# Delta rule on one Trainium2 core: the heads' inverses in groups of two, three and three heads in place of two groups of four

## The chip, the cores and the metric

The kernel runs on one core of one Trainium2 chip. The metric is the device time of one execution in microseconds (us), the median of several runs. The engines are PE (TensorE, matmuls), DVE (VectorE), ACT (ScalarE), POOL (GpSimd) and SP (SyncE, which issues all the DMAs of this kernel). Each engine executes its own instructions in the order in which the program holds them, and waits on semaphores for the others.

## What is computed

One inference step of a 4-layer encoder (pooling mixer, gated DeltaNet, stick-breaking attention, pooling mixer, each followed by a convolutional FFN) for two request groups that share the weights: 512 prompt frames and 64 frames of a running stream, 576 columns in all, in float32. The change lies in the DeltaNet mixer, which has 8 heads of width 128 and works in chunks of 64 frames:

```python
gc = jnp.cumsum(g, axis=-1)
kb = k * beta[..., None]
m = jnp.einsum('nbhid,nbhjd->nbhij', kb, k) * decay_strict
rhs = jnp.concatenate([v * beta[..., None], kb * jnp.exp(gc)[..., None]], axis=-1)
sol = lax.linalg.triangular_solve(eye + m, rhs, left_side=True, lower=True, unit_diagonal=True)
u, w = sol[..., :DV], sol[..., DV:]

def step(s, xs):
    u_c, w_c, qg_c, kg_c, attn_c, gl_c = xs
    v_new = u_c - jnp.einsum('bhck,bhkv->bhcv', w_c, s)
    o_c = jnp.einsum('bhck,bhkv->bhcv', qg_c, s) + jnp.einsum('bhij,bhjv->bhiv', attn_c, v_new)
    s = s * gl_c[..., None, None] + jnp.einsum('bhck,bhcv->bhkv', kg_c, v_new)
    return s, o_c
```

The kernel solves the triangular system by inverting `eye + m`. It takes the prompt in chunks of 128 frames (four) and the running stream in one of 64; the matrix of a chunk is cut into blocks of 32x32 on the diagonal, which are inverted on POOL, and larger inverses are put together from them by matmuls.

## The kernel before

**Planner.** The program is written by a planner (`Flow`) while it is built. Each piece of work is a Python generator that yields what it needs (tiles, free buffers, named events) and then emits instructions. `Flow.run` keeps a modelled clock for each engine and always goes on with the ready generator of the best priority. The order that results is fixed for PE, DVE, ACT, POOL and SP, and the chip executes it as written. A generator that yields `"@G"` is taken up again when POOL's modelled clock is within 250 ns, so that its POOL instructions come between those of others.

**The delta stage** (`dn`, from L1181) runs from about 440 us to 880 us of the span. A worker of the lowest priority emits 32 projections, matmuls of the normed input (split in a high and a low part) with a weight column block, in the order of the string `TN['order']` (L275): k0 q0 q1 k1 k2 q2 k3 q3 v2 v0 v1 v3 k4 q4 k5 k6 q6 k7 q5 q7 z1 z0 z2 z3 v5 v4 v6 v7 z4 z5 z7 z6. What else is ready goes between them:

- `conv` (L1313) follows every k, q and v projection: a memset and a copy on POOL for the first columns, an evacuation of PSUM on DVE, a scaling on ACT, two small copies of the last columns to `dn_so` on POOL, three taps on DVE (`a<-a,dn_cw,a`, 128x579), a tanh on ACT that overwrites the input, and a product on DVE.
- `mat(h)` (L1372) follows the conv of k: k times k on PE, norms and decays, the matrix M. SP stores its diagonal blocks into the DRAM tile `dM[g]` of the group and the whole of it into `Mt[h]`, seven DMAs, and the event `M{h}` is fired.
- `inverse(g)` (L1415) waits for the matrices of its four heads and for two of the eight `h` buffers (the weights use the same ones). It loads the 72 blocks of the group (18 a head) with a block on each partition, sets T to the unit matrix on POOL, and makes 31 steps of forward substitution, two POOL instructions each (a product into a `q` tile, a subtraction from T). ACT writes the transposed T, SP stores both, and `inv{g}` is fired.
- `merge(h)` (L1446) waits for `inv{g}`, loads the head's blocks in 16 DMAs and makes the full inverse U with 22 matmuls of 128 columns. Two U tiles exist at a time (class limit U), and one merge runs at a time (class limit mg).
- `v_post(h)` (L1486) turns v round after its conv; two results exist at a time (class limit v), kept until the end of `rec(h)`.
- `prep_rec(h)` (L1504) makes the decayed attention matrix and keys; it waits for the end of `rec(h-2)`.
- `rec(h)` (L1539) makes the recurrence over the five chunks, one head after the other with some overlap: it needs `prep_rec(h)`, U and v of its head.

The z projections gate the results, and the output projection follows. The trace puts nearly every instruction on L26, the line of the helper that calls the engine, so that groups are told apart by tiles: `h<-h,q` and `q<-h,h` on POOL are the steps of `inverse`, `dn_so<-a` the small copies of `conv`, `d<-a` on SP the stores of `mat`, `b` on DVE a finished k or q, `p` is PSUM.

Of the kernel before, what the change touches and what calls it, by code (L numbers as in the profile page):

```python
# [12 lines left out]
AF = mybir.ActivationFunctionType  # L13
ALU = mybir.AluOpType
# [275 lines left out]
class Step:  # L290
# [890 lines left out]
    def dn(self,l,st,nst,gnext):  # L1181
# [166 lines left out]
        def qk_post(h,i):  # L1348
            def g(P):
                if h not in kq:  # L1350
                    kq[h]=None
                    yield [("b",1)]
                    kq[h]=self.b().rearrange("p (l n) -> p l n",l=2)
                    f.fire(f"{st}:kq{h}")
                else: yield [f"{st}:kq{h}"]
                d=kq[h][:,i]
                c,C=yield from conv((8+h,h)[i],P,d)
                f.free(c)
                if i==0:
                    f.free(C)  # L1360
                    f.spawn(mat(h),TN['mat'])
                    return
                yield [d[:,:579],"@A"]
                A.activation(C[:,:579],d[:,:579],AF.Square)
                q=yield from sums(C,SO)
                f.free(C)
                V.tensor_scalar(out=eq[:,h],in0=q[:,:5],scalar1=4e-6,scalar2=1.28e-4,op0=ALU.add,op1=ALU.mult)
                f.free(q)
                f.fire(f"{st}:qn{h}")
            return g  # L1370

        def mat(h):  # L1372
            k=kq[h][:,0]
            yield [k[:,:579],("a",1,"M"),("p",2),("t",1)]
            M=self.a(cls="M"); r=self.s([128,5],F32,"t",8)
            p=self.p(); q=self.p()
            G.memset(r,1.0)
            for c in range(4): mm(p[:,cc[c]],k[:,cc[c]],k[:,cc[c]],start=True,stop=True)
            mm(q[:64,:64],k[:,ss],k[:,ss],start=True,stop=True)
            yield [p,q[:64,:64],r,"@V"]  # L1380
            for c in range(4): V.scalar_tensor_tensor(out=M[:,cc[c]],in0=p[:,cc[c]],scalar=1.0,in1=self.ident,op0=ALU.mult,op1=ALU.mult,accum_out=r[:,c:c+1])
            V.scalar_tensor_tensor(out=M[:64,sm],in0=q[:64,:64],scalar=1.0,in1=self.ident[:64,:64],op0=ALU.mult,op1=ALU.mult,accum_out=r[:64,4:5])
            V.tensor_scalar(out=r,in0=r,scalar1=4e-6,scalar2=None,op0=ALU.add)
            V.reciprocal(out=rk2[:,h],in_=r)
            G.tensor_tensor(out=r,in0=r,in1=mhalf,op=ALU.pow)
            yield [f"{st}:dec",("p",1)]
            p2=self.p()
            G.memset(M[64:128,sm],0.0)
            bank(h,self.mpos,p2,q,64)
            yield [r,rk2[:,h]]  # L1390
            V.tensor_tensor(out=nbk[:,h],in0=nbe[:,:,h],in1=rk2[:,h],op=ALU.mult)
            V.tensor_tensor(out=vsc[:,h],in0=beta[:,:,h],in1=r,op=ALU.mult)
            f.free(r)
            f.fire(f"{st}:kn{h}")
            yield [p2,q[:64,64:128],"@A"]
            for c in range(4): A.activation(M[:,cc[c]],p2[:,cc[c]],AF.Exp,scale=-1.0,bias=bE[:,c,h:h+1])
            A.activation(M[:64,sm],q[:64,64:128],AF.Exp,scale=-1.0,bias=bE[:64,4,h:h+1])
            f.free(p2)
            yield [M[:,:NT],"@V"]
            for c in range(4): V.scalar_tensor_tensor(out=M[:,cc[c]],in0=p[:,cc[c]],scalar=rk2[:,h,c:c+1],in1=M[:,cc[c]],op0=ALU.mult,op1=ALU.mult)  # L1400
            V.scalar_tensor_tensor(out=M[:64,sm],in0=q[:64,:64],scalar=rk2[:64,h,4:5],in1=M[:64,sm],op0=ALU.mult,op1=ALU.mult)
            f.free(p,q)
            g=h//4; o=18*(h%4)
            if g not in dM: dM[g]=self.dram([72,32,32])
            d=dM[g]
            yield [M[:,:NT]]
            for b in range(4):
                S.dma_start(out=d[o:o+16].rearrange("(c b) i j -> b i c j",b=4)[b],
                    in_=M[32*b:32*b+32,:512].rearrange("p (c j) -> p c j",j=128)[:,:,32*b:32*b+32])
            for b in range(2): S.dma_start(out=d[o+16+b],in_=M[32*b:32*b+32,512+32*b:544+32*b])  # L1410
            Mt[h]=self.dram([128,NT]); S.dma_start(out=Mt[h],in_=M[:,:NT])
            f.free(M)
            f.fire(f"{st}:M{h}")

        def inverse(g):  # L1415
            yield [f"{st}:M{h}" for h in range(4*g,4*g+4)]
            yield [("h",2),("q",1)]
            Bt,Tt=(self._t([128,1024],F32,"h") for _ in (0,1))
            v3=lambda t: t.rearrange("p (i j) -> p i j",j=32)
            MB,T=v3(Bt),v3(Tt)  # L1420
            S.dma_start(out=MB[:72],in_=dM[g])
            G.memset(Tt[:72],0.0); G.memset(Tt[:72,0:1024:33],1.0)
            prt=self.q()
            yield [Bt,Tt]
            for j in range(31):
                yield ["@G"]
                n=31-j; w=j+1
                pr=prt[:72,:n*w].rearrange("p (a b) -> p a b",b=w)
                G.tensor_tensor(out=pr,in0=MB[:72,j+1:,j:j+1].to_broadcast([72,n,w]),in1=T[:72,j:j+1,:w].to_broadcast([72,n,w]),op=ALU.mult)
                G.tensor_tensor(out=T[:72,j+1:,:w],in0=T[:72,j+1:,:w],in1=pr,op=ALU.subtract)  # L1430
            f.free(prt)
            yield [Tt,"@A"]
            A.activation(MB[:72],T[:72].rearrange("p i j -> p j i"),AF.Copy)
            r=[]
            for X in (Tt,Bt):
                d=self.dram([72,32,32])
                yield [X]
                S.dma_start(out=d,in_=X[:72])
                r.append(d)
            f.free(Bt,Tt)  # L1440
            TU[g]=r
            f.fire(f"{st}:inv{g}")
# [1 line left out]


        def merge(h):  # L1446
            g=h//4; hh=h%4
            yield [f"{st}:inv{g}",("a",3,"mg"),("a",1,"U")]
            P=self.a(cls="mg"); U=self.a(cls="U"); T=self.a(cls="mg"); M=self.a(cls="mg")
            for X in (P,U,T,M): G.memset(X[:,:NT],0.0)  # L1450
            D_=Mt.pop(h)
            for i in (0,64): S.dma_start(out=blk(P,0,512)[i+32:i+64,:,i:i+32],in_=blk(D_,0,512)[i+32:i+64,:,i:i+32])
            S.dma_start(out=P[32:64,512:544],in_=D_[32:64,512:544])
            for X,d in ((U,TU[g][1]),(T,TU[g][0])):
                for b in range(4): S.dma_start(out=blk(X,0,512)[32*b:32*b+32,:,32*b:32*b+32],in_=d[18*hh:18*hh+16].rearrange("(c b) i j -> b i c j",b=4)[b])
                for b in (0,1): S.dma_start(out=X[32*b:32*b+32,512+32*b:544+32*b],in_=d[18*hh+16+b])
            S.dma_start(out=blk(M,0,512)[64:128,:,0:64],in_=blk(D_,0,512)[64:128,:,0:64])
            yield [P[:,:NT],U[:,:NT],("p",2)]
            p=self.p(); q=self.p()
            for c in cc: mm(p[:,c],P[:,c],U[:,c],start=True,stop=True)  # L1460
            mm(q[:64,:64],P[:64,sm],U[:64,sm],start=True,stop=True)
            yield [p,q,"@A"]
            A.activation(P[:,:512],p,AF.Copy)
            A.activation(P[:64,sm],q[:64,:64],AF.Copy)
            yield [P,T[:,:NT]]
            for c in cc: mm(p[:,c],T[:,c],P[:,c],start=True,stop=True)
            mm(q[:64,:64],T[:64,sm],P[:64,sm],start=True,stop=True)
            yield [p,q,"@V"]
            V.tensor_tensor(out=U[:64,sm],in0=U[:64,sm],in1=q[:64,:64],op=ALU.subtract)
            V.tensor_tensor(out=U[:,:512],in0=U[:,:512],in1=p,op=ALU.subtract)  # L1470
            for c in cc: mm(q[:,c],P[:,c],T[:,c],start=True,stop=True)
            yield [q,"@V"]
            V.tensor_tensor(out=T[:,:512],in0=T[:,:512],in1=q,op=ALU.subtract)
            f.free(q)
            yield [U,M]
            for c in cc: mm(p[:,c],M[:,c],U[:,c],start=True,stop=True)
            yield [p,"@A"]
            A.activation(P[:,:512],p,AF.Copy)
            yield [P,T]
            for c in cc: mm(p[:,c],T[:,c],P[:,c],start=True,stop=True)  # L1480
            yield [p,"@V"]
            V.tensor_tensor(out=U[:,:512],in0=U[:,:512],in1=p,op=ALU.subtract)
            f.free(p,T,P,M)
            Uf[h]=U
            f.fire(f"{st}:U{h}")
# [164 lines left out]
        def z_(h): proj(24+h,z_post(h),TN['pz'])  # L1650
        for x in TN['order'].split(): dict(k=k_,q=q_,v=v_,z=z_)[x[0]](int(x[1:]))
        def chains():
            for g in (0,1): f.spawn(inverse(g),TN['inv'])
            for h in range(8):
                f.spawn(merge(h),TN['merge']); f.spawn(prep_rec(h),TN['prep']); f.spawn(rec(h),TN['rec'])
        chains()
# [381 lines left out]
```

## Time and profile before

| | us |
|---|---|
| median of 3 runs | 2518.58 |
| lowest and highest | 2518.18 and 2522.79 |
| profiled execution | 2525.03 |
| its span, first to last instruction | 2523.3 |
| PE busy | 2462.4 (98%) |
| PE weight loads busy | 2394.3 (95%) |
| DVE busy | 1924.9 (76%) |
| ACT busy | 1298.2 (51%) |
| POOL busy | 365.9 (15%) |
| mean granted TensorE clock | 0.986 |

Busy time is the union of an engine's instructions; PE's are pipelined, so a busy PE is not PE at its best. The granted clock is 1 at 2.4 GHz and 0.5 at 1.2 GHz. In the trace's views a row with a time begins with the start in us and the duration in us, then engine, line, operation, output<-inputs and the shapes; an idle time before it stands in square brackets with what ended it. A row of a group has, after the bar, the busy time in us and the mean duration in ns, then the idle time before its instructions and what ended it.

### The profile page before, as it was taken

Reading aid. Unit: us, or ns where it says so; the run is one execution under the profiler, and the core shown is the slowest. Engines: PE = TensorE matmul, PEld = TensorE weight load, DVE = VectorE, ACT = ScalarE, POOL = GpSimd, SP = SyncE. Lnnn points to the kernel's source line nnn. Section 1 sums busy time; section 2 is a strip of 40 time slices with the busy share of each in tenths; the row PEclk is TensorE's granted clock in tenths of the full one; section 3 lists DMA queues with packets and bytes.
Section 4 is the critical chain, followed back from the end, with each engine's and each line's share of the span. In section 5 each row is a group of like instructions: output and inputs, shape, how many; then the busy total and the mean of one; then the engine's idle time right before and its main releaser. Section 6 shows DMA issues by size and latency. Waiting matters only on the chain.

```text
span 2523.3 us, 46793 instructions
## 1 busy us (share of the span) xinstructions
PE 2462.4 (98%) x18337; PEld 2394.3 (95%) x18337; DVE 1924.9 (76%) x3727; ACT 1298.2 (51%) x2459; POOL 365.9 (15%) x734
## 2 busy tenths in 40 slices
PE   8989999998999999999999999999999999899998
PEld 7989999998999899999999888899999999899998
DVE  6988787887555479877885767779777788877776
ACT  6455544544344344444565667645444465544445
POOL 0000000138441001000001221200000001000000
PEclk9999999999999999999999999999999999999999
DMA  3223223332322222323233122222233231223231
GB/s 110 83 87 101 84 78 100 108 95 62 79 65 57 75 77 63 97 88 97 86 125 113 51 78 64 92 71 79 84 91 94 86 107 53 76 76 97 88 95 62
DMA packets 349056, 212.91 MB, mean 84 GB/s; under 512 B 30298, under 2 KB 341210, under 8 KB 348836
## 3 DMA queue, kind: packets, MB, share of 16 engines
q1 hardware_dynamic: 348836, 209.93, 28.3%
q8 instruction: 144, 2.36, 0.4%
q14 instruction: 76, 0.62, 0.1%
HBM read 192.41 MB, written 17.47 MB: 83 GB/s over the span
## 4 chain that ended last, share of the span: by engine, by line
PE 66%; DVE 2%; issue 1%; ACT 0%; POOL 0%; DVEq 0%; POOLq 0%; ACTq 0%
PE p L26 66%; DVE a L26 1%; DVE h L26 1%; DVE r L26 0%; ACT a L26 0%; DVE b L26 0%; ACT b L26 0%; POOL t L26 0%; DVE xl L26 0%; DVE q L26 0%; ACT xh L26 0%; DVEq L2034 0%; ACT q L26 0%; POOL rtf L26 0%; POOLq L2034 0%
## 5 line engine op out<-in xcount | busy, mean ns | idle before, releaser
L26 PE MATMUL p<-xh,h 128*128 128x288 f32 x4864 | 1040.6, 300 | 24.1 <-ACT xh L26 20.9
L26 PEld LDWEIGHTS p<-xh,h 128*128 128x128 f32 x4864 | 803.6, 189 | 31.1 <-ACT xh L26 22.2
L26 ACT ACTIVATE h<-r 128x512 fp32r<-128x512 f32 (+1 forms) x708 | 508.4, 739 | 420.1 <-PE p L26 320.9
L26 PE MATMUL p<-xl,h 128*128 128x288 f32 x2432 | 706.0, 297 | 1.6 <-DVE xl L26 1.6
L26 PE MATMUL p<-b,h 128*128 128x288 f32 x4992 | 681.0, 297 | 5.6 <-ACT b L26 3.0
L26 PEld LDWEIGHTS p<-b,h 128*128 128x128 f32 x4992 | 668.5, 189 | 9.3 <-DVE b L26 3.8
L26 DVE TENSOR_TENSOR h<-r,h 128x512 fp32r<-128x512 f32 (+1 forms) x708 | 580.7, 829 | 52.4 <-ACT h L26 51.3
L26 PEld LDWEIGHTS p<-xl,h 128*128 128x128 f32 x2432 | 461.6, 190 | 3.5 <-DVE xl L26 3.2
L26 DVE TENSOR_TENSOR a<-p,a 128x288 f32<-128x288 f32 (+6 forms) x650 | 265.8, 448 | 197.8 <-PE p L26 188.6
L26 PE MATMUL p<-a,h 128*128 128x288 f32 x2592 | 374.1, 299 | 0.0
L26 PEld LDWEIGHTS p<-a,h 128*128 128x128 f32 x2592 | 359.5, 192 | 0.0
L26 POOL COPY so<-a 128x2 f32<-128x2 f32 x176 | 100.2, 599 | 1513.5 <-DVE a L26 1513.5
L26 ACT ACTIVATE a<-a 128x512 f32<-128x512 f32 (+6 forms) x362 | 192.9, 555 | 133.8 <-DVE a L26 117.3
L26 ACT ACTIVATE q<-p 128x288 f32<-128x288 f32 x288 | 118.2, 410 | 185.3 <-PE p L26 181.5
L26 DVE SCALAR_TENSOR_TENSOR a<-a,fcw,a 128x578 f32<-128x578 f32 x176 | 144.2, 819 | 5.5
L26 DVE TENSOR_TENSOR a<-p,q 128x288 f32<-128x288 f32 (+2 forms) x216 | 70.5, 355 | 53.7 <-PE p L26 53.5
L26 ACT ACTIVATE b<-a 128x576 fp32r<-128x576 f32 x96 | 65.5, 682 | 81.7 <-DVE a L26 81.5
L26 POOL TENSOR_TENSOR a<-a,a 128x512 fp32r<-128x512 f32 (+1 forms) x64 | 67.3, 1052 | 252.5 <-DVE a L26 237.5
L26 DVE TENSOR_TENSOR r<-r 128x512 f32<-128x512 f32 x144 | 99.9, 694 | 4.3
L26 PE MATMUL p<-a,a 128*128 128x128 f32 (+10 forms) x656 | 102.8, 287 | 0.1
L26 ACT ACTIVATE xh<-a,gains 128x288 fp32r<-128x288 f32 (+2 forms) x128 | 66.3, 531 | 70.8 <-DVE a L26 70.3
L26 DVE TENSOR_TENSOR r<-r,r 128x512 f32<-128x512 f32 x144 | 99.0, 688 | 2.5
(192 smaller groups left out, 2424.7 us busy)
## 6 DMA issues: line engine op xcount, KB each, us to landing
r<-in_ffn_w_up_dram SPq DMA_DIRECT2D x176, 512.0 KB
r<-in_ffn_w_down_dram SPq DMA_DIRECT2D x80, 512.0 KB
r<-in_dn_w_in_dram SPq DMA_DIRECT2D x32, 512.0 KB
r<-in_sb_w_qkv_dram SPq DMA_DIRECT2D x24, 512.0 KB
d<-a SPq DMA_DIRECT2D x24, 288.0 KB
a<-d SPq DMA_DIRECT2D x16, 288.0 KB
r<-in_ffn_w_down_dram SPq DMA_DIRECT2D x16, 256.0 KB
r<-in_dn_w_out_dram SPq DMA_DIRECT2D x8, 512.0 KB
```

Source lines behind the costliest of these rows:

```text
L26: r = f(*a, **k)
```

## The change

The groups of `inverse` are no longer heads 0 to 3 and 4 to 7, but (0,1), (2,3,4) and (5,6,7). A helper gives for a head its group, its first block and the group's number of blocks; the tiles in DRAM and the partitions used become 36, 54 and 54 instead of 72 and 72. Three inverses are spawned instead of two. Nothing else differs, neither the order of the projections nor priorities and limits.

```diff
+        GR=((0,1),(2,3,4),(5,6,7))
+        def grp(h):
+            g=[h in x for x in GR].index(True)
+            return g,18*GR[g].index(h),18*len(GR[g])
...
-            g=h//4; o=18*(h%4)
-            if g not in dM: dM[g]=self.dram([72,32,32])
+            g,o,n=grp(h)
+            if g not in dM: dM[g]=self.dram([n,32,32])
...
         def inverse(g):
-            yield [f"{st}:M{h}" for h in range(4*g,4*g+4)]
+            n_=18*len(GR[g])
+            yield [f"{st}:M{h}" for h in GR[g]]
             yield [("h",2),("q",1)]
...
-            S.dma_start(out=MB[:72],in_=dM[g])
-            G.memset(Tt[:72],0.0); G.memset(Tt[:72,0:1024:33],1.0)
+            S.dma_start(out=MB[:n_],in_=dM[g])
+            G.memset(Tt[:n_],0.0); G.memset(Tt[:n_,0:1024:33],1.0)
...
-                pr=prt[:72,:n*w].rearrange("p (a b) -> p a b",b=w)
-                G.tensor_tensor(out=pr,in0=MB[:72,j+1:,j:j+1].to_broadcast([72,n,w]),in1=T[:72,j:j+1,:w].to_broadcast([72,n,w]),op=ALU.mult)
-                G.tensor_tensor(out=T[:72,j+1:,:w],in0=T[:72,j+1:,:w],in1=pr,op=ALU.subtract)
+                pr=prt[:n_,:n*w].rearrange("p (a b) -> p a b",b=w)
+                G.tensor_tensor(out=pr,in0=MB[:n_,j+1:,j:j+1].to_broadcast([n_,n,w]),in1=T[:n_,j:j+1,:w].to_broadcast([n_,n,w]),op=ALU.mult)
+                G.tensor_tensor(out=T[:n_,j+1:,:w],in0=T[:n_,j+1:,:w],in1=pr,op=ALU.subtract)
...
-            A.activation(MB[:72],T[:72].rearrange("p i j -> p j i"),AF.Copy)
+            A.activation(MB[:n_],T[:n_].rearrange("p i j -> p j i"),AF.Copy)
...
         def merge(h):
-            g=h//4; hh=h%4
+            g,o,_=grp(h)
...
-            for g in (0,1): f.spawn(inverse(g),TN['inv'])
+            for g in range(len(GR)): f.spawn(inverse(g),TN['inv'])
```

## Rows read from the trace of the kernel before

**Rows 1.** The page's first part: busy us (share of the span) and instructions of engines.

```profile
PE 2462.4 (98%) x18337; PEld 2394.3 (95%) x18337; DVE 1924.9 (76%) x3727; ACT 1298.2 (51%) x2459; POOL 365.9 (15%) x734
```

**Rows 2.** Stretches: length, busy PE, PEld, DVE, ACT, POOL; clock, DMA share, GB/s.

```profile
526.00:559.00 33.00, 33.00 (x258) 32.07 (x257) 27.93 (x76) 14.60 (x30) 10.53 (x25) 1.00 0.46 121
559.00:617.00 58.00, 51.74 (x374) 50.27 (x373) 41.87 (x84) 20.26 (x35) 53.20 (x95) 0.91 0.22 58
617.00:664.00 47.00, 45.60 (x350) 42.69 (x350) 33.49 (x89) 20.23 (x43) 12.88 (x28) 1.00 0.45 116
664.00:722.00 58.00, 56.09 (x440) 51.63 (x439) 28.84 (x59) 22.45 (x63) 44.62 (x80) 1.00 0.17 40
...
770.00:866.00 96.00, 95.49 (x732) 89.17 (x731) 50.33 (x102) 39.80 (x102) 12.06 (x29) 1.00 0.26 75
866.00:889.00 23.00, 19.54 (x127) 18.29 (x126) 10.12 (x24) 8.23 (x16) 1.34 (x3) 0.85 0.05 14
```

**Rows 3.** Shorter stretches of the same view, under the first inverse.

```profile
589.00:595.00 6.00, 0.21 (x2) 0.11 (x1) 4.51 (x6) 0.69 (x2) 5.69 (x8) 0.66 0.33 87
595.00:601.00 6.00, 6.00 (x27) 5.33 (x28) 4.42 (x19) 2.70 (x6) 5.50 (x13) 0.50 0.00 0
```

**Rows 4.** PE in order of time, the instruction after its idle time.

```profile
594.89 2.48 PE L26 MATMUL p<-b 128*128 128x128 f32 x10 [5.79 <-DVE b L26]
```

**Rows 5.** ACT in order of time, the tanh of that conv.

```profile
593.35 0.69 ACT L26 ACTIVATE a<-a 128x579 f32<-128x579 f32 x1 [4.35 <-POOL dn_so L26]
```

**Rows 6.** POOL in order of time: first inverse's first step, copies, both inverses' last steps.

```profile
559.14 0.75 POOL L26 TENSOR_TENSOR q<-h,h 72x31 f32<-72x31 f32 x1 [3.74 <-issue]
...
593.13 0.31 POOL L26 COPY dn_so<-a 128x3 f32<-128x3 f32 x2
...
615.49 0.25 POOL L26 TENSOR_TENSOR h<-h,q 72x31 f32<-72x31 f32 x1
...
720.76 0.25 POOL L26 TENSOR_TENSOR h<-h,q 72x31 f32<-72x31 f32 x1
```

**Rows 7.** Groups by line on POOL, 558 to 617, then 664 to 722.

```profile
L26 POOL TENSOR_TENSOR h<-h,q 72x31 f32<-72x31 f32 (+15 forms) x31 | 24.7, 798 | 2.4
L26 POOL TENSOR_TENSOR q<-h,h 72x31 f32<-72x31 f32 (+15 forms) x31 | 21.2, 684 | 5.2 <-issue 3.7
...
L26 POOL TENSOR_TENSOR h<-h,q 72x31 f32<-72x31 f32 (+15 forms) x31 | 18.4, 592 | 2.4
L26 POOL TENSOR_TENSOR q<-h,h 72x31 f32<-72x31 f32 (+15 forms) x31 | 18.2, 586 | 3.7 <-DMA h<-d 1.6
```

**Rows 8.** Conv taps on DVE by line: 526 to 560, 559:617, 617:664, 664:722.

```profile
L26 DVE SCALAR_TENSOR_TENSOR a<-a,dn_cw,a 128x579 f32<-128x579 f32 x12 | 9.8, 818 | 1.4 <-ACT a L26 1.1
...
L26 DVE SCALAR_TENSOR_TENSOR a<-a,dn_cw,a 128x579 f32<-128x579 f32 x18 | 17.3, 959 | 5.8 <-ACT a L26 5.4
...
L26 DVE SCALAR_TENSOR_TENSOR a<-a,dn_cw,a 128x579 f32<-128x579 f32 x12 | 9.8, 819 | 3.0 <-ACT a L26 2.7
...
L26 DVE SCALAR_TENSOR_TENSOR a<-a,dn_cw,a 128x579 f32<-128x579 f32 x3 | 2.5, 836 | 0.1
```

**Rows 9.** POOL by line and shape, 550 to 730: memsets.

```profile
L26 POOL MEMSET a<- 128x576 f32 x20 | 10.7, 575 | 0.3 <-DMA d<-h 0.2
...
L26 POOL MEMSET h<- 72x1024 f32 x2 | 1.9, 949 | 17.5 <-PE p L26 17.5
```

**Rows 10.** SP in order of time: stores of heads 1, 3, 4, 7; state load of rec(4).

```profile
520.82 3.17 SPq L26 DMA_DIRECT2D d<-a  x7
...
551.65 3.17 SPq L26 DMA_DIRECT2D d<-a  x7
...
602.59 3.17 SPq L26 DMA_DIRECT2D d<-a  x7
...
652.00 3.27 SPq L26 DMA_DIRECT2D d<-a  x7
...
779.67 0.53 SPq L26 DMA_DIRECT2D d<-in_state_dn_dram  x1
```

More of the change, by code (lines that the diff above doesn't have):

```diff
@@ L1427, in inverse @@
                 n=31-j; w=j+1
-                pr=prt[:72,:n*w].rearrange("p (a b) -> p a b",b=w)
-                G.tensor_tensor(out=pr,in0=MB[:72,j+1:,j:j+1].to_broadcast([72,n,w]),in1=T[:72,j:j+1,:w].to_broadcast([72,n,w]),op=ALU.mult)
-                G.tensor_tensor(out=T[:72,j+1:,:w],in0=T[:72,j+1:,:w],in1=pr,op=ALU.subtract)
+                pr=prt[:n_,:n*w].rearrange("p (a b) -> p a b",b=w)
+                G.tensor_tensor(out=pr,in0=MB[:n_,j+1:,j:j+1].to_broadcast([n_,n,w]),in1=T[:n_,j:j+1,:w].to_broadcast([n_,n,w]),op=ALU.mult)
+                G.tensor_tensor(out=T[:n_,j+1:,:w],in0=T[:n_,j+1:,:w],in1=pr,op=ALU.subtract)
             f.free(prt)
             yield [Tt,"@A"]
-            A.activation(MB[:72],T[:72].rearrange("p i j -> p j i"),AF.Copy)
+            A.activation(MB[:n_],T[:n_].rearrange("p i j -> p j i"),AF.Copy)
             r=[]
             for X in (Tt,Bt):
-                d=self.dram([72,32,32])
+                d=self.dram([n_,32,32])
                 yield [X]
-                S.dma_start(out=d,in_=X[:72])
+                S.dma_start(out=d,in_=X[:n_])
                 r.append(d)
@@ L1454, in merge @@
             for X,d in ((U,TU[g][1]),(T,TU[g][0])):
-                for b in range(4): S.dma_start(out=blk(X,0,512)[32*b:32*b+32,:,32*b:32*b+32],in_=d[18*hh:18*hh+16].rearrange("(c b) i j -> b i c j",b=4)[b])
-                for b in (0,1): S.dma_start(out=X[32*b:32*b+32,512+32*b:544+32*b],in_=d[18*hh+16+b])
+                for b in range(4): S.dma_start(out=blk(X,0,512)[32*b:32*b+32,:,32*b:32*b+32],in_=d[o:o+16].rearrange("(c b) i j -> b i c j",b=4)[b])
+                for b in (0,1): S.dma_start(out=X[32*b:32*b+32,512+32*b:544+32*b],in_=d[o+16+b])
             S.dma_start(out=blk(M,0,512)[64:128,:,0:64],in_=blk(D_,0,512)[64:128,:,0:64])
```

## The prediction

> **What bounds the kernel now.** I read the page's busy times first: TensorE (PE) is busy 98% of the span and nothing else comes near it [rows 1]. The change moves no matmul in or out, so it can only move the time in which PE waits or runs at the lower clock. Next I read the delta stage in stretches, cut at the two inverses [rows 2]. The reader is to see, in each stretch, its length less PE's busy time: 0.00 us in 526 to 559, 58.00 - 51.74 = 6.3 us while the first inverse runs (559 to 617), 1.4 us from 617 to 664, 1.9 us while the second runs (664 to 722), 0.5 us from 770 to 866 and 3.5 us at the end (866 to 889). That is all there is to win by idling less, about 13 us, and nearly half of it lies under the first inverse.
>
> The fine stretches say what that one costs [rows 3]: PE does next to nothing from 589 to 595 and then runs 595 to 601 at a granted clock of 0.50 (the lower level, 1.2 GHz), so 6.0 us of busy time do 3.0 us of work. 6.3 + 3.0 = 9.3 us.
>
> Why it stands there: PE's idle time of 5.79 us ends with DVE's write of a `b` tile, the k row of head 4, which `mat(4)` multiplies [rows 4]. Going back, the tanh of that conv on ACT waited 4.35 us for POOL [rows 5], and on POOL the two small copies of `conv` end at 593.44, queued between steps of the inverse [rows 6]. POOL executes in the written order, and the inverse's steps took longer there than the order allowed for. The same 62 instructions are 24.7 + 21.2 = 45.9 us in the first inverse and 18.4 + 18.2 = 36.6 us in the second [rows 7]. DVE's conv taps (two SBUF inputs of 579 columns) tell the two apart: 17.3 us of them beside the first, 2.5 us beside the second, and they too are longer beside an inverse, 959 ns against 818 and 819 without one [rows 8]. So an inverse among convs makes POOL late, POOL makes the convs late, and PE, which stands in written order, waits.
>
> **The change part by part.** *The work.* A third inverse is 62 more element-wise instructions on POOL, two memsets, one load, two stores and one ACT copy. A group now has 36 or 54 partitions instead of 72. No row has these steps at fewer partitions; the nearest are memsets, 575 ns for 128x576 and 949 ns for 72x1024 [rows 9], 1.00 and 0.93 ns a column: price goes by columns. Bounds: half (36/72) to all of 45.9 us; I take all, as the memset rows do. POOL thus gets 37 to 46 us more and PE nothing.
>
> *Where the three stand.* The first inverse began 559.14 - 551.65 = 7.5 us after SP began the store of head 3's matrix [rows 6, 10] and lasted to 615.74, 56.6 us. The two-head group needs head 1, stored from 520.82 [rows 10]: it runs from about 528 to 585. The middle group needs head 4, stored from 602.59: about 610 to 666. The last needs head 7, stored from 652.00, and a free POOL: about 667 to 723, where the second one ended already (721.0 [rows 6]). So heads 0 and 1 gain 30 us, head 4 gains 55, heads 2 and 3 lose 50, heads 5 to 7 stand still.
>
> *What the gain is worth: nothing by itself.* `rec(4)` loads its state at 779.67 [rows 10], nearly 60 us after the inverse of its head: it waits for v4, the 26th of 32 projections in the fixed order. `rec(1)` waits for the end of `rec(0)` (two v slots, taken by v2 and v0). PE is full meanwhile, 95.49 of 96 us from 770 to 866 [rows 2], so recurrences done sooner only change places with projections.
>
> *What the three cost PE.* Price each place by its conv taps, as a share of the stretch [rows 8]: 17.3/58 = 0.30 under the first inverse (9.3 us), 2.5/58 = 0.04 under the second (1.9 us). The two-head group falls on 528 to 585; the row for 526 to 560 gives 9.8/34 = 0.29, as dear as the first: 9.3 us. It moves the stall rather than removing it: the convs of k3, q3, v2 and v0 now stand among its steps. The middle group falls on 610 to 666; 617 to 664 has 9.8/47 = 0.21, that is 0.65 of the way: 1.9 + 0.65 x 7.4 = 6.7 us, bounds 1.9 and 9.3. The last stays at 1.9. Sum after: 9.3 + 6.7 + 1.9 = 17.9 us; before, 9.3 + 1.4 + 1.9 = 12.6. The change costs 5.3 us.
>
> That the two slow each other is shown by 959 against 818 ns [rows 8]. The Trainium skill (SBUF — State Buffer, "Who interferes with whom") has VectorE and GpSimd share one port pair under an exclusive lock, which a VectorE instruction with two SBUF inputs contends for and one that reads PSUM beside one SBUF input does not. By that rule conv taps are the right measure. By VectorE's busy share alone (27.93/33 = 0.85, 0.72 and 0.50 [rows 2]) the two-head group would cost 9.3 + 0.13/0.22 x 7.4 = 13.7 us, and the change 9.7 us instead of 5.3.
>
> *The queues.* SP's stores of an inverse wait for its end, and the weight loads behind them too; this now happens three times. I cost it at nothing: weights are loaded several projections ahead, and no idle time of PE in these rows ends with a weight. If that cover failed, a third block would be worth at most POOL's lateness, 45.9 - 36.6 = 9.3 us. ACT's transposing copy also waits for the inverse; its cost is within the prices above. An inverse takes two of the eight `h` buffers for its time, as it did, for 57 us more.
>
> **The rivals.** *The middle inverse is as cheap as the second was.* Then 9.3 + 1.9 + 1.9 against 12.6: +0.5 us, 2519. For it: from 617 to 664 PE lost only 1.4 us though convs ran. Against it: no inverse ran then.
>
> *The stall goes, faster.* The two-head group ends near 585, before the conv of k4 has its POOL copies (593 now), so `mat(4)` would find its k in time; if k3, q3, v2 and v0 have enough slack, all three cost 1.9 us: 5.7 - 12.6 = -6.9 us, 2512. For it: PE lost 0.00 us from 526 to 559. Against it: there was no inverse, and POOL was busy 10.53 of 33 us only.
>
> *Work moved in front of v4, slower.* With heads 2 to 4 done together, `rec(3)` can end sooner, so that `merge(5)` and `prep_rec(5)`, which wait for it, come before v4's projection instead of after it. They push v4, and with it the chain of four recurrences to the end of the stage. About 40 matmuls of 128 columns; ten of them took 2.48 us at half clock [rows 4], so 1.24 each ten at full: 5 us. It decides if that chain, not the amount of matmuls, sets the end, as the 3.5 us idle after 866 [rows 2] suggest in part. With the forecast's 5.3 it is +10.3, 2529.
>
> **How the numbers follow.** The profiled execution took 2525.03 us, span 2523.3 and 1.7 around it, 6.45 above the median of 2518.58; the sum of +5.3 gives 2530.3 against the former and 2523.9 against the median, which is the prediction. About 0.2% (5 us) is what a measurement can tell from no change, so the forecast stands on the edge. Forecast 0.38 (its own range 2520 to 2529; slower 0.28, same 0.10); cheap middle 0.25 (same 0.22, faster 0.03); stall gone 0.24 (faster 0.22, same 0.02); v4 pushed 0.13 (slower). Faster 0.25, same 0.34, slower 0.41. The range takes in the rivals and the bounds, with half of the 3.5 us idle at the end more or less: from -6.9 - 1.7 = -8.6 (stall gone) to 9.3 + 9.3 + 1.9 - 12.6 + 5 + 1.7 = +14.6 (middle at its upper bound, v4 pushed): 2510 to 2533.
>
> **What would show it.** Right: POOL busy by 37 to 46 us more in the stage; a PE wait of some us between 540 and 585 that ends with DVE, behind a conv whose POOL copies stand among inverse steps; a second one between 610 and 666; `rec(4)` again right after v4's conv. Wrong, faster: no half-clock stretch between 530 and 670. Wrong, slower: no new wait there, but the end of the stage later by itself. A middle inverse of 37 us on POOL instead of some 43 would break the price by conv taps; steps of the two-head group at half the time would break the price by columns.

## The result and the profile after

The changed kernel takes 2535.48 us (median of 4, 2532.22 to 2538.01) against 2520.64 for the kernel before in the same rounds: 1.0058 times, interval 1.004 to 1.0077, 15 us slower. The forecast was slower, by 5.3 us, with a range up to 2533. The profiled execution of the changed kernel took 2533.43 us, span 2531.6. That is only 8.4 us more than the profiled execution of the kernel before, although the delta stage ends 13 us later: behind that stage the instructions are the same, and they took 1629.6 us here and 1634.3 in the trace before. So the two traces are compared inside the stage.

The page's first part answers [rows 1]. PE has the same 18337 matmuls and nearly the same busy time; POOL has 64 instructions and 44 us more.

```profile
PE 2464.3 (97%) x18337; PEld 2395.6 (95%) x18337; DVE 1926.5 (76%) x3727; ACT 1300.5 (51%) x2460; POOL 409.8 (16%) x798
```

The stretches answer [rows 2, 3], cut at the three inverses as they came to stand; the columns are the same. The last four are short ones within them.

```profile
528.00:592.00 64.00, 57.17 (x421) 55.69 (x421) 45.89 (x86) 22.92 (x46) 59.26 (x99) 0.97 0.30 81
592.00:616.00 24.00, 19.32 (x133) 18.05 (x132) 16.22 (x40) 10.80 (x17) 7.26 (x18) 0.86 0.41 104
616.00:684.00 68.00, 66.65 (x511) 61.94 (x510) 44.83 (x125) 27.98 (x70) 54.24 (x100) 0.97 0.19 49
684.00:698.00 14.00, 11.68 (x60) 10.98 (x60) 4.24 (x10) 5.76 (x15) 2.36 (x4) 0.66 0.43 107
698.00:757.00 59.00, 58.77 (x454) 54.89 (x454) 33.04 (x61) 22.63 (x55) 47.54 (x82) 0.99 0.23 56
...
783.00:879.00 96.00, 95.45 (x728) 88.92 (x727) 49.63 (x100) 39.98 (x103) 11.52 (x25) 1.00 0.27 78
879.00:902.00 23.00, 19.52 (x129) 18.28 (x129) 10.20 (x23) 8.23 (x16) 1.34 (x3) 0.85 0.06 15
...
576.00:580.00 4.00, 4.00 (x21) 3.96 (x20) 1.94 (x4) 2.40 (x6) 3.61 (x9) 0.59 0.00 0
...
602.00:607.00 5.00, 5.00 (x22) 4.33 (x23) 2.43 (x18) 0.61 (x2) 1.31 (x2) 0.54 0.58 142
660.00:666.00 6.00, 6.00 (x35) 5.62 (x34) 3.50 (x5) 1.93 (x8) 5.53 (x10) 0.72 0.37 96
...
688.00:699.00 11.00, 11.00 (x55) 10.52 (x54) 3.77 (x9) 1.76 (x4) 0.57 (x1) 0.53 0.28 69
```

The reader is to see that the end of the stage is nearly the same as before, 3.48 us idle in its last 23 and 0.55 in the 96 ahead of them, moved by 13 us. All that is new lies from 528 to 699. While the two-head group's steps run (528 to 592), PE idles 6.83 us and half clock takes 4 x 0.41 = 1.6 more; behind their end (592 to 616) it idles 4.68 us and half clock takes 5 x 0.46 = 2.3: 8.5 + 7.0 = 15.5. While the middle group's steps run (616 to 684), PE idles 1.35 us and half clock takes 6 x 0.28 = 1.7; behind their end it idles 2.32 us and half clock takes 11 x 0.47 = 5.2: 3.0 + 7.5 = 10.5. The last one has 0.2. Together 26.2 us against 12.6 before, 13.6 more, which is the measured loss but for 1 us. More than half of the 26.2, 14.5 us, stands behind the ends of the first two inverses.

PE in order of time answers [rows 4]; these are the waits of half a microsecond or more from 540 to 700.

```profile
546.02 1.39 PE L26 MATMUL p<-b 128*128 128x128 f32 x10 [1.83 <-DVE b L26]
550.33 0.30 PE L26 MATMUL p<-a,dn_idr 128*128 128x64 f32 x1 [0.66 <-DVE a L26]
559.14 1.02 PE L26 MATMUL p<-ones,a 128*128 128x1 f32 x8 [1.20 <-POOL q L26]
565.45 0.73 PE L26 MATMUL p<-c_ident,a 128*128 128x128 f32 x5 [0.88 <-DVE a L26]
575.64 1.16 PE L26 MATMUL p<-c_ident,a 128*128 128x128 f32 x5 [2.26 <-DVE a L26]
601.86 2.48 PE L26 MATMUL p<-b 128*128 128x128 f32 x10 [4.68 <-DVE b L26]
...
687.64 1.72 PE L26 MATMUL p<-b 128*128 128x128 f32 x10 [2.32 <-ACT a L26]
```

Where the first inverse before made PE wait once, the two-head group does so five times among its steps, for k of head 3 (546, and once more at 550), a norm of q (559) and two v (565, 575), and once behind its end, for k of head 4 (602). ACT, POOL and DVE show the two paths. The first is ACT's scaling of a conv (552.09), which waits for POOL's two instructions ahead of it. The second starts at the inverse's end (ACT at 592.14).

```profile
552.09 0.78 ACT L26 ACTIVATE a<-a,dn_cw 128x579 f32<-128x579 f32 x1 [6.33 <-POOL a L26]
...
592.14 2.11 ACT L26 ACTIVATE h<-h 36x1024 f32<-36x1024 f32 x1 [3.02 <-POOL h L26]
594.14 0.68 ACT L26 ACTIVATE a<-a 128x579 f32<-128x579 f32 x1
...
683.18 2.15 ACT L26 ACTIVATE h<-h 54x1024 f32<-54x1024 f32 x1 [1.56 <-POOL h L26]
```

```profile
534.55 0.61 POOL L26 TENSOR_TENSOR q<-h,h 36x31 f32<-36x31 f32 x1 [0.18 <-POOL dn_so L26]
...
551.83 0.09 POOL L26 MEMSET a<- 128x3 f32 x1
551.87 0.18 POOL L26 COPY a<-dn_st 128x3 f32<-128x3 f32 x1
...
591.87 0.24 POOL L26 TENSOR_TENSOR h<-h,q 36x31 f32<-36x31 f32 x1
```

```profile
594.86 0.76 DVE L26 SCALAR_TENSOR_TENSOR a<-a,a 128x579 f32<-128x579 f32 x1 [3.17 <-ACT a L26]
595.54 0.88 DVE L26 TENSOR_TENSOR a<-p,a 128x288 f32<-128x288 f32 x3
```

On the first path the conv's memset and copy stand behind 11 pairs of steps, and ACT waits 6.33 us for 0.27 us of work. On the second path the written order puts ACT's transposing copy ahead of the tanh of v3's conv (594.14). ACT waits 3.02 us for POOL's last step, the tanh comes behind the copy, DVE waits 3.17 us for the tanh, and only then takes k of head 4 out of PSUM (595.54), for which PE waits 4.68 us. How much of this is the copy's and how much the late conv of v3 (its taps ended at 591.69), no run tells apart. The wait before 687.64 stands behind the middle group's transposing copy in the same way. The first inverse took 592.11 - 534.55 = 57.6 us, about as long with 36 partitions as the first one before with 72 (56.6 [rows 6]).

### The profile page after: what moved, and what is told of

The parts are those of the page before. It is cut to its first block, busy times and chain, and to the rows that moved or that the text cites. A ratio compares the mean times of both kernels' runs of the same rounds, so it can differ in the third digit from the quotient of the medians.

```text
span 2531.6 us, 46843 instructions
## 1 busy us (share of the span) xinstructions
PE 2464.3 (97%) x18337; PEld 2395.6 (95%) x18337; DVE 1926.5 (76%) x3727; ACT 1300.5 (51%) x2460; POOL 409.8 (16%) x798
## 4 chain that ended last, share of the span: by engine, by line
PE 87%; POOL 5%; DVE 3%; issue 2%; ACT 1%; DMA 1%; SPq 0%; DVEq 0%; POOLq 0%; ACTq 0%
PE p L26 87%; POOL h L26 2%; POOL q L26 2%; DVE a L26 1%; DVE h L26 1%; POOL t L26 0%; ACT a L26 0%; DMA b<-in_x_prompt_dram 0%; DVE r L26 0%; DMA h<-d 0%; ACT xh L26 0%; POOL dn_so L26 0%; DVE b L26 0%; ACT h L26 0%; POOL a L26 0%
## 5 line engine op out<-in xcount | busy, mean ns | idle before, releaser
L26 ACT ACTIVATE a<-p 128x448 f32<-128x448 f32 (+5 forms) x149 | 65.1, 454 | 74.2 <-PE p L26 65.8
```

Of the source, the lines that this page charges most:

```text
L26: r = f(*a, **k)
```

## The experiments

Theory: POOL needs longer for an inverse among convs than the planner's model says, so that what the written order places behind it comes late, and PE, in its own written order, waits for that. Rivals: the written order itself costs the time (work moved in front of v4); an inverse more costs the same wherever it stands; POOL is too busy there for any order.

**Steps of one element, in an unchanged order.** The new helper `narrow` tells the planner the full shapes and emits the instruction with small ones, so that these kernels leave the inverses out:

```diff
-                G.tensor_tensor(out=T[:n_,j+1:,:w],in0=T[:n_,j+1:,:w],in1=pr,op=ALU.subtract)
+                G.narrow("tensor_tensor",dict(out=T[:n_,j+1:,:w],in0=T[:n_,j+1:,:w],in1=pr,op=ALU.subtract),
+                    dict(out=T[:n_,j+1:j+2,:1],in0=T[:n_,j+1:j+2,:1],in1=pr[:,:1,:1],op=ALU.subtract))
```

(and the product likewise, in all inverses)

> The changed kernel in the same written order, but each of the 186 step instructions of its three inverses works on one element instead of its full shape (so the inverses are left out, and with them that part of the result); the planner still charges the full shape. Theory lateness (POOL's real length makes the convs late and PE waits): the idle time and half clock of 11.5 + 4.1 us in the first inverse's place and about 10 us around the second's end go, as does what they cost before: about 2511 us, 10 under the kernel before. Rival order (the written order itself, recurrences and merges in front of v4, costs the 15 us): about 2532 to 2535, no gain.

> The kernel before in its own written order, each of the 124 step instructions of its two inverses on one element (the inverses are left out). Lateness: the 9.3 us under the first inverse go, about 2511 us, and the two kernels with such steps lie within 3 us of each other. Order: also about 2511, but the kernel with three groups some 14 us above it.

Measured: 2510.44 and 2509.96 us, the kernel before 2522.32 beside them (0.9959, interval 0.9944 to 0.9974, and 0.9958, 0.9943 to 0.9973). The order of the three groups costs 0.5 us, nothing that can be told from none: this rival falls. POOL's steps in that order cost 2535.5 - 2510.4 = 25 us (27 if each kernel is taken against the kernel before beside it), and 2522.3 - 2510.0 = 12 us in the old one. These are the traces' sums, 26.2 and 12.6. The steps on POOL and two stretches, first of the changed kernel, then of the same with small steps:

```profile
L26 POOL TENSOR_TENSOR h<-h,q 36x31 f32<-36x31 f32 (+23 forms) x93 | 66.9, 719 | 7.3
L26 POOL TENSOR_TENSOR q<-h,h 36x31 f32<-36x31 f32 (+23 forms) x93 | 61.0, 656 | 8.7 <-DMA h<-d 3.4 <-POOL dn_so L26 0.2
...
L38 POOL TENSOR_TENSOR q<-h,h 54x1 f32<-54x1 f32 (+1 forms) x93 | 30.9, 332 | 12.4 <-DMA h<-d 7.2
L38 POOL TENSOR_TENSOR h<-h,q 54x1 f32<-54x1 f32 (+1 forms) x93 | 29.6, 318 | 7.3
```

```profile
520.00:600.00 80.00, 70.35 (x519) 67.92 (x517) 57.69 (x116) 32.56 (x65) 63.79 (x110) 0.98 0.31 81
600.00:700.00 100.00, 94.47 (x674) 88.02 (x675) 61.11 (x169) 39.43 (x96) 60.83 (x116) 0.90 0.27 70
...
520.00:600.00 80.00, 79.06 (x606) 76.73 (x605) 64.80 (x147) 37.93 (x76) 45.75 (x116) 1.00 0.41 107
600.00:700.00 100.00, 98.13 (x764) 91.58 (x763) 60.19 (x159) 43.65 (x103) 47.64 (x157) 1.00 0.26 66
```

The steps still take 60.5 us on POOL, against 127.9 in the changed kernel, but PE idles 0.9 + 1.9 us from 520 to 700 and the clock stays at 1.00.

**One group at a time.** The same edit, under `if g in (0,)` and `if g in (1,)`.

> The changed kernel in its written order, the steps of the two-head group alone on one element each (its inverse is left out). If the losses of the inverses add up, as the idle and half-clock time of the trace do (about 15.6 us up to 607, 10.3 around the middle group's end): 2535 - 15 = 2520. If the first stall only takes over what a later one would cost: 2528 or more.

> The same with the steps of the middle group alone on one element each (its inverse is left out). Adding up: 2535 - 10 = 2525. If the middle one costs what the prediction gave it, 6.7: 2529. If it costs nothing: 2535.

Measured: 2514.7 and 2528.87 (before 2521.73; 0.9972, 0.996 to 0.9984, and 1.003, 1.002 to 1.0041). Without the two-head group's steps 21 us go, without the middle one's 6.6. The two nearly add up to the 25, but part of what stood at the middle group's place hangs on the first: with the first one's steps small, the middle and the last cost 2514.7 - 2510.4 = 4.3 us in place of 10.7 (roughly, for the executions of that kernel lie between 2510.03 and 2522.51). Its trace says which part. PE waits at the middle group's end as long as in the changed kernel:

```profile
675.34 1.42 PE L26 MATMUL p<-b 128*128 128x128 f32 x10 [2.37 <-ACT a L26]
```

But the granted clock is 1.00 from 612 to 690, so that the half clock behind this wait is not paid; why it is not, no run shows. With the middle group's steps small instead, ACT does not wait for POOL ahead of the transposing copy, and PE's wait there is 0.78 us in place of 2.32, shorter by about what ACT had waited (1.56). "A first stall only takes over a later one's cost" is wrong, the opposite holds in part.

**The place.** One more wait in `inverse`, and another grouping:

```diff
-            yield [f"{st}:M{h}" for h in GR[g]]
+            yield [f"{st}:M{h}" for h in GR[g]]+([f"{st}:M3"] if g==0 else [])
```

```diff
-        GR=((0,1),(2,3,4),(5,6,7))
+        GR=((0,1,2,3),(4,5),(6,7))
```

> The changed kernel with one more wait in the planner: the two-head group is taken up only when head 3's matrix is stored, as the first inverse was before. Lateness with place: the first inverse costs 9 us again instead of about 15, the middle one about 10, so 2527 to 2530. Rival place does not matter (every inverse more costs the same): 2535.

> Three inverses too, but groups (0,1,2,3), (4,5), (6,7): the first as before, the third among few convs. Lateness with place: the first costs 9 us as before, the second (from about 640) some 2 to 7, the third under 2: 2521 to 2526. Rival (an inverse more costs about 15 us wherever it stands): 2535.

Measured: 2528.11 (1.0019, 1.0008 to 1.0031) and 2521.89 (1.0003, 0.9993 to 1.0012), before 2522.32. Three inverses cost 15, 6 or 0 us more than two, by where they stand (each with the order that the planner then writes): the rival of a fixed price falls. In groups of 4, 2 and 2 the second and third ran from 636 to 744 and PE lost 3.3 us in that stretch:

```profile
636.00:760.00 124.00, 120.74 (x934) 111.16 (x934) 66.56 (x142) 53.36 (x129) 95.36 (x172) 1.00 0.27 66
```

**The convs' small instructions on ACT.**

```diff
-            G.memset(C[:,0:3],0.0); G.tensor_copy(C[:,515:518],cst_[:,t::24])
+            A.activation(C[:,0:3],self.ones[:,0:3],AF.Copy,scale=0.0); A.activation(C[:,515:518],cst_[:,t::24],AF.Copy)
...
-            G.tensor_copy(so[:,0:3,t],C[:,512:515]); G.tensor_copy(so[:,3:6,t],C[:,579:582])
+            A.activation(so[:,0:3,t],C[:,512:515],AF.Copy); A.activation(so[:,3:6,t],C[:,579:582],AF.Copy)
```

> The changed kernel with the four small instructions of every conv (zeroing and copying the first columns, copying the last columns out) on ACT instead of POOL, so that no conv waits in POOL's queue; the planner writes a new order. If PE's stalls come through these copies: most of the 25 us go, 2512 to 2518. If they come through POOL's other work (norms of mat, buffers) or through DVE being slowed: 2530 or more.

> The kernel before with the same move to ACT. Through these copies: the 12 us that its inverses cost go but for a rest, 2510 to 2515, which would beat both kernels. Otherwise 2520 to 2525, or more if ACT's 96 further small instructions get in the way.

Measured: 2528.53 (1.0027, 1.0015 to 1.0039) and 2525.28 (1.0014, 1.0004 to 1.0023), before 2521.73. Seven of the 25 us go in the one, and in the other the time even rises by 3.5. So the copies are one path of several; what they cost by themselves is not shown, since the planner writes a new order and ACT has 96 more small instructions. With this edit the kernel with two groups shows two more paths, on ACT, on DVE and on PE:

```profile
615.65 1.98 ACT L26 ACTIVATE h<-h 72x1024 f32<-72x1024 f32 x1 [7.18 <-POOL h L26]
```

```profile
591.13 3.51 DVE L26 SCALAR_TENSOR_TENSOR a<-a,dn_cw,a 128x579 f32<-128x579 f32 x3
...
618.24 0.76 DVE L26 SCALAR_TENSOR_TENSOR b<-a,a 128x579 f32<-128x579 f32 x1 [6.52 <-ACT a L26]
```

```profile
596.53 2.07 PE L26 MATMUL p<-b 128*128 128x128 f32 x10 [3.71 <-DVE b L26]
619.14 1.19 PE L26 MATMUL p<-b 128*128 128x128 f32 x4 [4.04 <-DVE b L26]
```

ACT's transposing copy waits 7.18 us for the inverse's end, with the next tanh behind it, and three conv taps take 3.51 us where three of 819 ns [rows 8] would be 2.46. With three groups the largest wait, 4.19 us before 596.79, ended with a merge's load, again an inverse's end that came later than placed.

**An order that knows.** The planner charges 149 ns and 2.1 ns a column for an instruction of a step, 32.2 us for the 62 of one inverse. The first inverse before took 45.9 us [rows 7], (45.9 - 32.2)/31 = 0.44 us more for each of the 31 pairs. Only the planner's clock is changed, no instruction:

```diff
-                G.tensor_tensor(out=T[:n_,j+1:,:w],in0=T[:n_,j+1:,:w],in1=pr,op=ALU.subtract)
+                G.tensor_tensor(out=T[:n_,j+1:,:w],in0=T[:n_,j+1:,:w],in1=pr,op=ALU.subtract); f.clk["G"]+=440
```

(`told_more_4_4`: 800 ns)

> The changed kernel whose planner adds 0.44 us to POOL's modelled clock after each of the inverses' 93 steps, near what the chip takes more than modelled among convs; the instructions are the same, the written order follows the longer model. Theory: the loss comes from POOL being later than the order allows for, so an order that allows for it gets most of the 25 us back though POOL works as long as before: 2512 to 2520. Rival (POOL is simply too busy there, or DVE is slowed by sharing with it, whatever the order): 2530 or more.

> The kernel before with the same 0.44 us in the planner's model of each of its 62 steps. Theory: 8 to 12 us of the 12 that its inverses cost come back, 2510 to 2515, below both kernels. Rival: 2520 to 2525.

> Groups (0,1,2,3), (4,5), (6,7) with the same 0.44 us in the model. Theory: 2510 to 2516, like told_4_4; a third inverse is then free. Rival: 2522 or more.

> The kernel before with 0.80 us a step instead of 0.44: the model is now longer than the chip. Theory: no stall of PE under an inverse that ends with DVE behind a conv; the inverses end earlier than planned, so merges come later than they could: about the same as told_4_4, 2510 to 2516. Rival: as told_4_4 under its rival, 2520 or more.

Measured, with 2520.44 for the kernel before: 2510.66 (0.9956, 0.9941 to 0.9971), 2509.8 (0.9955, 0.9938 to 0.9971), 2510.69 (0.9959, 0.9944 to 0.9974) and 2518.94 (0.9994, 0.9984 to 1.0003). The changed kernel's 25 us come back while POOL works as long as before. The steps and two stretches with three groups:

```profile
L26 POOL TENSOR_TENSOR h<-h,q 36x31 f32<-36x31 f32 (+23 forms) x93 | 66.8, 718 | 7.3
L26 POOL TENSOR_TENSOR q<-h,h 36x31 f32<-36x31 f32 (+23 forms) x93 | 63.1, 678 | 6.3 <-DMA h<-d 1.5
```

```profile
520.00:600.00 80.00, 75.33 (x571) 72.79 (x570) 64.78 (x136) 36.43 (x71) 68.14 (x116) 1.00 0.32 86
600.00:700.00 100.00, 99.26 (x778) 93.82 (x778) 67.03 (x164) 44.02 (x105) 70.80 (x128) 1.00 0.27 70
```

129.9 us of steps against 127.9, yet PE's idle time from 520 to 700 falls from 15.2 us (80 - 70.35 and 100 - 94.47 in the changed kernel) to 5.4 and the clock stays at 1.00. DVE's conv taps take as long as well, 900 ns on the mean from 520 to 760 against 890, so that slower taps by themselves do not cost PE its time. The rival of a POOL too busy for any order falls. All three groupings end within 1 us of each other, 10 us below the kernel before, and level with the kernels that had small steps. The fourth run missed its expectation: with a model that is too long, its longest wait under the inverses is 0.89 us, as expected, but the merges come later (the fourth one's loads begin at 725.54 against 707.58 with 440 ns) and the last recurrences have less beside them. The stage's last wait of over 1 us ends at 879.99 against 869.53. From 840 to 900 PE is busy 53.09 us against 58.24, which is 5 of the 9 us; the first row is from the kernel with 800 ns:

```profile
840.00:900.00 60.00, 53.09 (x375) 48.52 (x374) 27.75 (x61) 20.14 (x48) 3.23 (x6) 0.97 0.26 82
```

```profile
840.00:900.00 60.00, 58.24 (x437) 57.21 (x436) 30.84 (x62) 21.61 (x44) 2.51 (x4) 0.97 0.34 106
```

## Why the prediction was right and wrong

The direction came and the size did not: 5.3 us forecast, 13.6 in the trace, 15 measured. Term by term, the two-head group cost 6.2 us more than its price, the middle one 3.8 more, the last one 1.7 less.

*What bounds the kernel, and that sooner recurrences are worth nothing:* right. With small steps the two orders differ by 0.5 us, `rec(4)` loads its state at 791.04, later by 11.4 us like all of the stage's end, and the rows of that end are nearly the same. The rival of work pushed in front of v4 is refuted by the same pair of runs. Where the three stand was less well foreseen: they ran from 535 to 592, 620 to 683 and 702 to 757, the last one about 35 us later than forecast, at a cost of 0.2 us.

*The mechanism:* right in kind. POOL comes late, what hangs on it comes late, and PE waits, shown by taking POOL's length away and by writing it into the plan. But the prediction followed it on one path only, through the convs' small instructions on POOL.

*Price by columns and not by partitions:* right. A product of 256 columns took 0.64 us with 36 partitions and 0.64 us with 72, the first row after, the second before:

```profile
563.83 0.64 POOL L26 TENSOR_TENSOR q<-h,h 36x256 f32<-36x256 f32 x1
...
689.18 0.64 POOL L26 TENSOR_TENSOR q<-h,h 72x256 f32<-72x256 f32 x1
```

*The price of the two-head group, 9.3 us, with ACT's transposing copy "within the prices above":* the step that failed. The trace has 15.5 there, and without its steps 21 us went, the half clock at the middle group's end with them. The price was taken from the first inverse before, by the share of conv taps, and that share came out as assumed (19.7 us of taps in 64 us, 0.31). While the steps ran, the cost was 8.5 us, near the price, though in five waits and not in one. What the price did not hold is the inverse's end: 7.0 us came behind it, by the chain through ACT's transposing copy. Behind the end of the first inverse before, PE lost 1.4 us at most (617 to 664 [rows 2]), so the figure from there had next to nothing of this. The rival in which the stall goes had it that `mat(4)` finds its k in time, since the inverse ends before k4's conv has its POOL copies; the inverse did end before (592.11), and PE waited 4.68 us for that k all the same, through ACT.

*The price of the middle group, 6.7 us:* the same step failed. The trace has 3.0 us while the steps ran and 7.5 behind their end; 6.6 us went when its steps alone were made small. That this is the 6.7 of the sum is luck, since the price was put on the convs among the steps and most of the cost stands behind the end.

*The last group, 1.9 us:* it was 0.2.

*SP's stores at nothing:* no wait of PE of half a microsecond or more between 540 and 700 ended with a weight, as said.

*The other measure, VectorE's busy share:* its 9.7 us came nearer than 5.3, but not by its reasoning. The two-head group had a busy share of 45.89/64 = 0.72, as the first inverse before, and not the 0.85 that gave 13.7. Nor was it carried through: the middle group at 33.49/47 = 0.71 would have cost about 9.0 by it, and the change 12.

*The range:* its upper end, +14.6, holds 5 us for a rival that did not come. For the three inverses alone it allowed 9.3 + 9.3 + 1.9 - 12.6 = 7.9 us, because 9.3 was taken as the dearest that an inverse could be.

## What to carry to other kernels

Where the order of all engines is written ahead, an engine that the model believes faster than it is costs most where many short waits of the bounding engine hang on it. Count the consumers, among the work and behind its end, where another engine's queue may hold an instruction that waits for the whole of it. Do not take one price from a place that had one of them. Before more or smaller pieces are tried, compare the modelled with the measured time of each engine's work in the trace, in its real neighbourhood: 0.44 us for each pair of step instructions, written into the plan, gave 10 us here with each of three groupings, while 0.80 gave nothing that can be told from none. Taking the length out of an instruction under an unchanged order tells lateness from order in two runs.

## What the runs showed of the hardware

POOL's steps and DVE's taps lengthen each other. The steps took 36.6 us where few taps ran and 45.9 among them [rows 7], taps 819 ns alone, 959 beside the first inverse and 1170 in the three shown above (3.51 / 3). With steps of one element in an unchanged order the taps from 520 to 700 took 819 ns on the mean, against 894 in the changed kernel. The Trainium skill (SBUF — State Buffer, "Who interferes with whom") has the two engines take turns on one port pair; the trace agrees in kind, and no run here isolates a single pair of instructions.

The clock fell to half not only after idle time. From 660 to 666 PE was busy 6.00 of 6 us by the trace and the granted clock was 0.72 on the mean (0.50 from 662 to 664); ahead of it stood matmuls of 1, 64 and 128 columns among projections, and no wait longer than 0.4 us. And a wait of 2.32 us before 687.64 was followed by 11 us at 0.53, dearer than the wait itself, while a wait of 2.37 us at the same place in the kernel whose first group had small steps was followed by a clock of 1.00.

A step instruction of one element still took 0.32 to 0.33 us on POOL on the mean, about half of the 0.66 to 0.72 of the full ones.
